# Another order of tasks in the mixer, at the first layer's end and in w_out of a hybrid decoder layer

## The chip, the cores and the metric

The kernel runs on one core of a Trainium2 chip. What counts is device time in microseconds (us) of one launch. The core has a matrix engine (TensorE, in the profile PE, with its weight loads as PEld), a vector engine (VectorE, DVE), a scalar engine (ScalarE, ACT), GpSimd (POOL) and a queue of transfers that SyncE (SP) issues. Each works through its own list of instructions in order, and they meet at semaphores.

## What is computed

One decoder layer on 512 tokens of width 1024, all in float32: a half-weighted SwiGLU feed-forward layer, a mixer of three branches, a projection `w_out`, and a second half-weighted feed-forward layer. Every step has a norm ahead of it and one behind it.

```python
x = x + 0.5 * rms_norm(swiglu(rms_norm(x)), ffn1_post)
u = rms_norm(x)
nsa_q, nsa_kv, nsa_g, dn_qkv, dn_a, dn_b, dn_z, mem_q = split(u @ w_in)
# NSA: compressed keys, selected blocks and window, 8 heads of 64
# DeltaNet: conv and silu of dn_qkv, then the chunked rule of 4 heads (chunks of 64):
#   a_mat = strict(beta * k k^T * decay) + I; solve a_mat against v and k; scan over chunks
#   o_dn = rms_norm(o_dn) * silu(dn_z)
# memory: cross attention of mem_q into 256 memory tokens
merged = sum(sigmoid(u @ w_gate[b]) * (o_b @ w_branch[b]) for b in 3 branches)
x = x + rms_norm(merged @ w_out)
x = x + 0.5 * rms_norm(swiglu(rms_norm(x)), ffn2_post)
```

## The kernel before

A float32 product is made of three products of rounded parts: every weight tile of 128x512 is loaded (`wraw`, in w_out `woraw`), ScalarE casts it to its high part `whi` (L106), VectorE or GpSimd subtracts that from the tile and leaves the low part `wlo` (L109), and TensorE multiplies high by high, low by high and high by low (L117 to L119, helper `mm3`). So each loaded tile costs a transfer, a cast, a subtraction and a dozen or so matmuls. `wload` holds four raw tiles in most stages; a load waits on SyncE's queue until one is free.

The program is a list of small tasks. `tasks` goes through lists of names in the table `PRM`, and calls one function for each name; the scheduler of the framework then interleaves their instructions, keeping what comes first in the lists ahead where it can. Three kinds of entry steer it: the lists (`order` for the mixer's first part, `order2` for attention and merge, `order0` for the first feed-forward layer's end, `order3` for w_out, `order_s` for the start), an offset of priority for a name (`off`, `off2` and so on), and for a name the number n such that every n-th low part goes to GpSimd instead of VectorE (`pool`, `pool3`; 0 is none).

The names in `order` that matter here: `c` is a product with `w_dn` and the convolution of one head and one of q, k, v (L185, L612: `cacc` from the product `pfm`); `h` its transposes and norm (`ptr`, then `rsqrt` L129 to L139, then `kn` or `qs`, then `ptk`); `k`, `r` and `l` make the tables of a head (`LT` is the lower triangle, from `pkk`); `z` is the product with `w_z`; `b` solves the triangle's 16x16 blocks for two heads at once: `LT` goes to DRAM (`dL`), comes back as `Lb`, 15 pairs of small VectorE steps (L719, L721) work on `Bi`, L722 turns it, and the result goes out (`dD`, from ScalarE's queue) and comes back as `Dc` (SyncE's queue, L726); `e` spreads `Dc` to `Dm` and `DT` (L739); `d` doubles the blocks in three levels (`pt`, `px`, `pxt`); `s` is the scan over chunks (`pst`, `pod`); `o` the output norm and its transposes (`on` L823, `pot` L824); `x` the tokens of the compressed keys (product with `w_cmp`, then 8 steps `X`, L900), `p` their hidden layer (`phid`, L917); `q` a product with `w_q`.

In `order0`: `k` and `v` are products with the memory's weights (`mem_k` gives `pfm`, `mem_v` gives `pmv`), each left by a copy on ScalarE (`mkv`, L517); `p`, `n`, `t` are post-norm, pre-norm (sum of squares on ScalarE, L152) and transposes (`ptr`, L166) of a half of the tokens. In `order3`: `s` splits the merged sum, `d` i h is half h of w_out's columns for token half i (accumulators `acc_mm` for d00, `acc_o` and `acc_r` for d01, `acc_e` for d10, `acc_s` for d11), and `p`, `n`, `t` are as above.

Of the kernel before, what the change touches and what calls it, by code (L numbers as in the profile page):

```python
# [33 lines left out]
PAD = 88  # L34


PRM = {'order': ['i', 'a', 'w', 'c01', 'h01', 'c00', 'c10', 'c02', 'r0', 'h00', 'h02', 'c12', 'k0', 'h10', 'c22', 'l0', 'c11', 'h11', 'h12', 'r1', 'z', 'k1', 'c21', 'l1', 'h22', 'b0', 'c20', 'h21', 'e0', 'r2', 'h20', 'c32', 'l2', 'c31', 'd00', 'h31', 'k2', 'r3', 'c30', 'd01', 'l3', 'b1', 'd02', 'x0', 's00', 'e1', 'd10', 'h32', 'x1', 'd11', 'h30', 's01', 's02', 's03', 'q0', 'p0', 'o0', 'k3', 'p1', 'q3', 'p2', 'p3', 'd12', 's10', 'p4', 'q1', 'p5', 's11', 'p6', 'p7', 's12', 'q2', 'f', 's13', 'o1'], 'dma': {'l': 'sync', 'b': 'sync', 'd': 'scalar', 'c': 'sync', 'r': 'sync'}, 'off': {'b0': 300, 'h31': 400, 'h00': 20, 'r1': 50, 'h32': 50, 'h11': 200, 'h12': 200, 'd10': 100, 'A01': 100, 'A10': 100, 'A11': 100, 'A20': 100, 'A31': 100, 'A21': 200, 'x0': 20, 'x1': 20, 'C2': 50, 'L': 200, 'S310': 400, 'S001': 20, 'S311': 400, 'A30': 100, 'r0': 400, 'd02': 20, 's11': 50, 'V20': 400, 'l3': 100, 'q1': 20, 'f': 400, 'l1': 20, 'h20': 100, 'h22': 100, 'r3': 50, 'P010': 100, 'y': 100, 'h02': 50, 'S101': 20, 'A00': 100, 'Q0': 50, 'Q1': 50, 'Q2': 50, 'Q3': 50, 'P110': 400, 'V31': 50, 'd01': 200, 'o0': 400, 'p0': 50, 'p1': 50, 'p2': 50, 'p4': 50, 'p5': 50, 'p6': 50, 'p7': 50, 'b1': 20, 'h01': 100, 'M15': 20, 'P201': 400, 'e0': 100, 'e1': 100, 'o1': 20, 'q0': 50, 'q2': 20, 'h21': 20, 'd11': 50, 'p3': 50}, 'ph': 'e', 'po': 'ss', 'xpd': (0, 1, 2), 'order2': ['K1', 'K0', 'B', 'M10', 'C3', 'Q0', 'C0', 'Q1', 'S000', 'S001', 'P001', 'C1', 'P000', 'S010', 'C2', 'S011', 'V00', 'P010', 'S100', 'P011', 'S110', 'Q2', 'V01', 'P100', 'S101', 'W0', 'P101', 'S111', 'Q3', 'M12', 'V10', 'P110', 'S200', 'P111', 'S210', 'V11', 'P200', 'M14', 'S201', 'M15', 'P201', 'S211', 'W1', 'V20', 'P210', 'M11', 'P211', 'V21', 'S301', 'S300', 'W2', 'P301', 'S311', 'P300', 'L', 'M13', 'S310', 'G0', 'V30', 'P310', 'G2', 'M16', 'P311', 'V31', 'W3', 'A00', 'M00', 'M17', 'A01', 'G1', 'U0', 'A10', 'M05', 'A11', 'G3', 'A30', 'A31', 'U1', 'U3', 'M03', 'A20', 'A21', 'U2', 'M07', 'M22', 'M02', 'M20', 'M24', 'M06', 'M27', 'M21', 'M01', 'M26', 'M23', 'M04', 'M25'], 'order0': ['d0', 'p0', 'n0', 't0', 'd1', 'k2', 'k0', 'p2', 'p3', 'k1', 'n1', 'v', 'k3', 't1'], 'order3': ['s2', 's3', 's7', 's6', 's1', 's5', 's0', 's4', 'd01', 'd00', 'g', 'p0', 'd10', 'n0', 't0', 'd11', 'p1', 'n1'], 't3': (('mm', 'r'), ('e', 's')), 'pool': {'W2': 2, 's13': 3, 'k0': 0, 'k1': 0, 'k2': 0, 'k3': 2, 'p3': 1, 'C0': 0, 'C1': 0, 'C2': 0, 'C3': 2, 'S310': 0, 'L': 3, 'd11': 3, 'p0': 1, 'p1': 1, 'p2': 1, 'p4': 2, 'p5': 1, 'p6': 1, 'p7': 1, 'S311': 0, 'h01': 0, 'h00': 0, 'h02': 0, 'h10': 0, 'h11': 0, 'h12': 0, 'h22': 0, 'h21': 0, 'h20': 0, 'h31': 0, 'h30': 3, 'h32': 0, 'i': 2, 'P011': 2, 'c21': 0, 'd01': 2, 'S000': 0, 'S001': 0, 'S010': 0, 'S011': 0, 'S100': 0, 'S101': 0, 'S110': 0, 'S111': 0, 'S200': 0, 'S201': 0, 'S210': 0, 'S211': 0, 'S300': 0, 'S301': 0, 'M24': 2, 'G2': 2, 'A01': 0, 'M10': 2, 'M15': 2, 'M12': 2, 'M14': 2, 'M13': 2, 'M17': 2, 'M11': 2, 'M16': 2, 'M23': 0, 'M27': 3, 'M01': 2, 'M00': 2, 'M03': 0, 'M07': 2, 'M06': 0, 'M22': 2, 'M04': 2, 'M20': 2, 'M26': 3, 'M02': 0, 'M21': 2, 'M25': 2, 'M05': 2, 'c11': 1, 'o1': 3, 'P000': 2, 'P001': 1, 'P010': 2, 'P100': 2, 'P101': 2, 'P110': 2, 'P111': 2, 'P200': 2, 'P201': 2, 'P210': 2, 'P211': 2, 'P301': 0, 'P300': 2, 'P310': 2, 'P311': 2, 'c12': 0, 'b1': 1, 'x0': 0, 'x1': 0, 'V21': 0, 'c30': 0, 'c01': 0, 'c02': 0, 'c00': 0, 'c10': 0, 'c22': 0, 'c20': 0, 'c31': 0, 'c32': 0, 's01': 3, 'A31': 0, 'd12': 0, 'y': 2, 'G0': 2, 'G1': 2, 'G3': 2, 'U3': 0, 'W3': 2, 'r1': 2, 's12': 3, 'U2': 0, 'Q0': 2, 'Q1': 2, 'Q2': 2, 'Q3': 1, 's00': 3, 's02': 2, 's03': 3, 's10': 3, 's11': 3, 'e1': 2, 'd00': 1, 'U0': 0, 'U1': 0, 'l2': 0}, 'pool3': {'d00': 3, 'd01': 3, 'd10': 3, 'd11': 3, 'p1': 2, 't1': 3, 't0': 3, 's5': 2, 's7': 2, 's1': 2, 's0': 2, 's3': 2, 's6': 2, 's2': 2, 's4': 2, 'q0': 1}, 'pool0': {}, 'off0': {'p3': 20, 'n1': 50, 't1': 100}, 'off3': {'s1': 20, 's5': 200, 'g': 200, 't0': 400}, 'tt': ('e', 's'), 'order_s': ['t00', 'w10', 'w00', 'y', 't01', 't02', 'w01', 't03', 'w11', 'R0', 'F000', 'x', 'F101', 'n', 'F200', 't10', 't11', 't12', 't13', 'c', 'F110', 'B', 'F211', 'F011'], 't0': ('e', 's'), 'rs': ((0, 0), (0, 0)), 'ra': (1, 1), 'warm': 8, 'pools': {'F000': 0, 'F101': 0, 'F200': 0, 'F011': 0, 'F110': 0, 'F211': 0, 'w10': 0, 'w11': 0, 't00': 0, 't01': 0, 't02': 0, 't03': 0, 't13': 0, 't10': 0, 't11': 0, 't12': 0, 'w00': 0, 'w01': 0}, 'ptc': 'vvs', 'cva': 'v', 'offs': {'t13': 100, 'R1': 400}, 'vnc': 's', 'sp3': 0, 'hsc': 'vv', 'sf2': 2, 'psc': 'vvvv', 'sp1': 0, 'vbs': 'v', 't1c': 'vs', 'sgv': 256}


class Body:  # L40
    def __init__(self, ctx, tc, a, out, tap):
# [17 lines left out]
        pw = self.bank("o", "warm")  # L59
        for _ in range(PRM.get("warm", 10)):  # L60
            nc.tensor.matmul(pw, wm[:, :P], wm, start=True, stop=True)
# [204 lines left out]
    def ffn_tile(self, n, f, t, xh, xl, RB, H, banks=None, tags=("mm", "mm"), pre=None):  # L266
# [14 lines left out]
        if r:  # L281
            (nc.vector if w <= PRM["sgv"] else nc.gpsimd).tensor_tensor(sg[:, :r], sg[:, :r], RB, op=OP.mult)
        return nc.vector.tensor_tensor(H[:, f, t], sg, pu, op=OP.mult)
# [320 lines left out]
    def dn_conv(self, h, s, uh, ul):  # L604
# [4 lines left out]
        ac = self.tp.tile([P, SEQ], F32, tag="tmpa", bufs=2, name="cacc")  # L609
        self.scale(PRM.get("cva", "s"), ac, p, self.cw[:, j, 3:4])  # L610
        for i in range(3):
# [11 lines left out]
    def dn_head(self, h, s, y, sc, dp, d):  # L623
# [7 lines left out]
        if s == 2:  # L631
            d["vb"] = dp.tile(T4, F32, tag="vb", name="vb", bufs=4)
            if PRM.get("vbs", "v") == "v":
                v.tensor_tensor(d["vb"], p, beta[:, :, h, None].to_broadcast(T4), op=OP.mult)
# [11 lines left out]
        n = self.da.tile(T4, F32, tag="kn", name="kn", bufs=1) if s else self.tp.tile(T4, F32, tag="tmpb", name="qs", bufs=2)  # L646
        if PRM.get("hsc", "vv")[s] == "v":
            v.tensor_tensor(n, p, r[:, :, None].to_broadcast(T4), op=OP.mult)
# [53 lines left out]
    def dma(self, k):  # L702
        return getattr(self.nc, PRM.get("dma", {}).get(k, "sync"))

# [789 lines left out]
```

## Time and profile before

| | |
|---|---|
| three runs | 1382.18, 1367.98, 1378.45 us; median 1378.45 |
| profiled execution | 1365.18 us, its span 1363.4 us |
| PE busy | 1332.1 us (98%) |
| DVE, ACT, POOL busy | 897.0, 719.1, 146.1 us |
| mean granted TensorE clock | 0.996 |

The span runs from the first to the last instruction; the execution's own time has 1.8 us around it. The stages lie so: the first feed-forward layer to 370, memory products and norms to 397, the mixer's first part to 638, attention and merge to 955, w_out to 1004, the second feed-forward layer to the end. The first head pair's blocks are solved at 486 to 521, the second's at 541 to 575.

### The profile page before, as it was taken

Reading aid. Unit: us, or ns where it says so; the run is one execution under the profiler, and the core shown is the slowest. Engines: PE = TensorE matmul, PEld = TensorE weight load, DVE = VectorE, ACT = ScalarE, POOL = GpSimd, SP = SyncE. Lnnn points to the kernel's source line nnn. Section 1 sums busy time; section 2 is a strip of 40 time slices with the busy share of each in tenths; the row PEclk is TensorE's granted clock in tenths of the full one; section 3 lists DMA queues with packets and bytes.
Section 4 is the critical chain, followed back from the end, with each engine's and each line's share of the span. In section 5 each row is a group of like instructions: output and inputs, shape, how many; then the busy total and the mean of one; then the engine's idle time right before and its main releaser. Section 6 shows DMA issues by size and latency. Waiting matters only on the chain.

```text
span 1363.4 us, 21808 instructions
## 1 busy us (share of the span) xinstructions
PE 1332.1 (98%) x7839; PEld 1130.3 (83%) x7839; DVE 897.0 (66%) x1797; ACT 719.1 (53%) x1542; POOL 146.1 (11%) x132
## 2 busy tenths in 40 slices
PE   9999999999999999999999999999999999999997
PEld 8889999787887878677777777888788899998886
DVE  6897875777558576646876424223587778766765
ACT  7556664766555553216654334323585565646643
POOL 0020000000011312003110121333300000000000
PEclk9999999999999999999999999999999999999999
DMA  7643331676654332423121222532744433317673
GB/s 254 194 147 109 109 110 32 209 244 209 190 176 125 98 100 63 113 82 118 46 63 47 70 63 92 164 100 93 243 136 148 134 121 98 121 33 261 194 224 101
DMA packets 107453, 178.32 MB, mean 131 GB/s; under 512 B 18908, under 2 KB 28496, under 8 KB 107344
## 3 DMA queue, kind: packets, MB, share of 16 engines
q1 hardware_dynamic: 107056, 176.67, 41.8%
q8 instruction: 61, 1.00, 0.3%
q14 instruction: 48, 0.39, 0.1%
q10 hardware_dynamic: 288, 0.26, 0.1%
HBM read 166.84 MB, written 10.01 MB: 130 GB/s over the span
## 4 chain that ended last, share of the span: by engine, by line
PE 49%; DVE 3%; ACT 1%; issue 1%; DVEq 0%; ACTq 0%
PE pfm L119 5%; PE pfm L117 5%; PE pfm L118 5%; PE smm L406 5%; PE se L406 3%; PE po L1051 2%; PE ss L406 2%; PE ps L1019 2%; PE ppt L1039 1%; PE acc_mm L117 1%; PE acc_mm L118 1%; PE acc_mm L119 1%; PE acc_e L118 1%; PE acc_e L117 1%; PE acc_e L119 1%; PE acc_s L117 1%
## 5 line engine op out<-in xcount | busy, mean ns | idle before, releaser
L106 ACT CAST whi<-wraw 128x512 fp32r<-128x512 f32 (+1 forms) x314 | 189.8, 616 | 185.3 <-PE pfm L119 70.3
L109 DVE TENSOR_TENSOR wlo<-wraw,whi 128x512 fp32r<-128x512 f32 (+1 forms) x270 | 184.1, 690 | 143.6 <-ACT whi L106 139.6
L118 PE MATMUL pfm<-xth,wlo 128*128 128x512 f32 x384 | 154.9, 405 | 2.6 <-DVE wlo L109 2.6
L117 PE MATMUL pfm<-xth,whi 128*128 128x512 f32 x384 | 155.7, 406 | 1.1 <-DVE drz L134 0.7
L119 PE MATMUL pfm<-xtl,whi 128*128 128x512 f32 x384 | 154.0, 402 | 0.0
L118 PEld LDWEIGHTS pfm<-xth,wlo 128*128 128x128 f32 x384 | 72.3, 189 | 19.3 <-DVE wlo L109 3.2
L117 PEld LDWEIGHTS pfm<-xth,whi 128*128 128x128 f32 x384 | 72.4, 189 | 18.5 <-issue 3.9
L119 PEld LDWEIGHTS pfm<-xtl,whi 128*128 128x128 f32 x384 | 72.4, 189 | 15.4 <-issue 1.0
L109 POOL TENSOR_TENSOR wlo<-wraw,whi 128x512 fp32r<-128x512 f32 (+1 forms) x41 | 51.1, 1246 | 243.0 <-ACT whi L106 196.4
L106 ACT CAST ringh<-ringr 128x512 fp32r<-128x512 f32 x82 | 50.1, 620 | 42.4 <-DMA ringr<-in_ffn_d_dram 11.2
L406 PE MATMUL smm<-thi,fset 128*128 128x256 f32 x384 | 69.5, 279 | 0.0
L109 DVE TENSOR_TENSOR wlo<-ringr,ringh 128x512 fp32r<-128x512 f32 x75 | 51.4, 689 | 21.8 <-PE acc_e L119 8.7
L406 PEld LDWEIGHTS smm<-thi,fset 128*128 128x128 f32 x384 | 58.5, 188 | 0.2
L422 DVE TENSOR_TENSOR up<-smm,s 128x256 f32<-128x256 f32 x32 | 13.6, 424 | 67.2 <-ACT se L419 67.2
L406 PE MATMUL smm<-thi,fxtl 128*128 128x256 f32 x192 | 53.6, 279 | 0.6 <-DVE fxtl L388 0.6
L406 PE MATMUL smm<-thi,fxth 128*128 128x256 f32 x192 | 53.3, 278 | 0.0
L406 PE MATMUL se<-thi,fset 128*128 128x256 f32 x256 | 46.7, 280 | 0.0
L1022 ACT ACTIVATE Pm<-Pm,nm 128x128 f32<-128x128 f32 (+1 forms) x64 | 35.6, 557 | 11.9 <-DVE nm L1021 11.6
L258 POOL TENSOR_TENSOR xb<-xb,pre 128x512 f32<-128x512 f32 x2 | 2.5, 1277 | 356.7 <-ACT pre L257 356.7
L123 DVE TENSOR_TENSOR Hl<-H,Hh 128x256 fp32r<-128x256 f32 x88 | 35.0, 420 | 7.0 <-ACT Hh L122 5.5
L406 PEld LDWEIGHTS se<-thi,fset 128*128 128x128 f32 x256 | 39.1, 187 | 0.0
L379 DVE TENSOR_TENSOR fs<-fq 128x1024 f32<-128x1024 f32 x32 | 38.9, 1217 | 0.0
(550 smaller groups left out, 3979.3 us busy)
## 6 DMA issues: line engine op xcount, KB each, us to landing
wraw<-in_ffn_d_dram SPq DMA_DIRECT2D x94, 256.0 KB, 2.9
ringr<-in_ffn_d_dram SPq DMA_DIRECT2D x82, 256.0 KB, 2.9
fq<-in_ffn_g_dram SPq DMA_DIRECT2D x64, 256.0 KB, 2.9
fq<-in_ffn_u_dram SPq DMA_DIRECT2D x64, 256.0 KB, 2.7
wraw<-in_w_gate_dram SPq DMA_DIRECT2D x48, 256.0 KB, 2.8
wraw<-in_ffn_u_dram SPq DMA_DIRECT2D x34, 256.0 KB, 3.2
wraw<-in_ffn_g_dram SPq DMA_DIRECT2D x34, 256.0 KB, 3.5
woraw<-in_w_out_dram SPq DMA_DIRECT2D x32, 256.0 KB, 2.9
```

The lines of the kernel that those rows point to most:

```text
L106: nc.scalar.copy(hi, raw)
L109: eng.tensor_tensor(lo, raw, hi.bitcast(F32), op=OP.subtract)
L117: t.matmul(out, lh, rh, start=first, stop=False)
L118: t.matmul(out, ll, rh, start=False, stop=False)
L119: t.matmul(out, lh, rl, start=False, stop=last)
L123: return self.nc.vector.tensor_tensor(lo, src, hi.bitcast(F32), op=OP.subtract)
L379: add = lambda *x: v.tensor_tensor(*x, op=OP.add)
L406: m = lambda x, y, **kw: te.matmul(out, x, y, skip_group_check=True, **kw)
L1019: te.matmul(s[:, : max(n, 256)], A[:, qb * P : qb * P + P], K[j][:, : max(n, 256)], start=j == 0, stop=j == 1)
L1022: nc.scalar.activation(pm, pm, AF.Exp, bias=nm[:, qb : qb + 1], scale=-1.0, accum_out=sm[:, qb : qb + 1])
L1039: te.transpose(pt[:, o : o + P], Pm[:, self.OFF[qb] + kb * P : self.OFF[qb] + kb * P + P], self.ident)
L1051: te.matmul(po[64 * g : 64 * g + 64, kb * P :], vt[:, kb, br * P + 64 * g : br * P + 64 * g + 64], pts[g][:, col[kb] : col[kb] + n], start ...
```

## The change

It changes the table and nothing else. The tasks, their tiles and their arithmetic stay; the order of their instructions, and in a few products which engine subtracts, are others. The lists, cut to what moves most (the rest of the line is the table's other entries):

```diff
-'l0', 'c11', 'h11', 'h12', 'r1', 'z', 'k1', 'c21', 'l1', 'h22', 'b0', 'c20', 'h21', 'e0',
+'c11', 'h12', 'h11', 'h22', 'r1', 'k1', 'l1', 'b0', 'c21', 'z', 'h21', 'e0', 'c20',
...
-'k2', 'r3', 'c30', 'd01', 'l3', 'b1', 'd02', 'x0', 's00', 'e1', 'd10', 'h32', 'x1', 'd11',
+'k2', 'r3', 'd01', 'l3', 'b1', 'd02', 'x0', 's00', 'e1', 'd10', 'c30', 'h32', 'x1', 'd11',
...
-'q0', 'p0', 'o0', 'k3', 'p1', 'q3', 'p2', 'p3', 'd12',
+'q0', 'q3', 'p0', 'o0', 'p1', 'p2', 'p3', 'k3', 'd12',
...
-'order0': ['d0', 'p0', 'n0', 't0', 'd1', 'k2', 'k0', 'p2', 'p3', 'k1', 'n1', 'v', 'k3', 't1']
+'order0': ['d0', 'p0', 'n0', 't0', 'd1', 'k2', 'k0', 'p2', 'p3', 'v', 'k3', 'n1', 'k1', 't1']
...
-'order3': ['s2', 's3', 's7', 's6', 's1', 's5', 's0', 's4', 'd01', 'd00', 'g', 'p0', 'd10', 'n0', 't0', 'd11', 'p1', 'n1']
+'order3': ['s3', 's7', 's2', 's6', 's1', 's5', 's0', 's4', 'd00', 'd01', 'd11', 'g', 'p0', 'n0', 't0', 'd10', 'p1', 'n1']
...
-'off0': {'p3': 20, 'n1': 50, 't1': 100}, 'off3': {'s1': 20, 's5': 200, 'g': 200, 't0': 400}
+'off0': {'p3': 20, 'n1': 50, 'd0': 200, 'k2': 400, 'k1': 400}, 'off3': {'s1': 20, 's5': 200, 'g': 200, 't0': 400, 'd10': 200, 'p0': 200}
```

`order2` has about twenty names moved by one to five places; in `off` the offsets of `b1`, `s00`, `Q1`, `M14` rise to 200, of `A20` and `P011` to 400; `offs` gives two weight loads and transposes of the start an offset. In `pool` the names `h00`, `d02` and `V00` get 2, `K1` 3, `C0`, `M10` and `M06` 1, `G3` and `V11` 0; in `pool3` `d11` goes from 3 to 0. GpSimd subtracts for 51 tiles before and for 50 now (10 and 7 of them in w_out).

VectorE at the first head pair's blocks (`b0`), the last steps. Before:

```order
L719 TENSOR_TENSOR Bt<-Lb,Bi 64x28
L129 TENSOR_SCALAR drm<-dss 128x4
L612 SCALAR_TENSOR_TENSOR cacc<-pfm,cw,cacc 128x509
L721 TENSOR_TENSOR Bi<-Bi,Bt 64x2x14
L130 TENSOR_SCALAR dry<-drm 128x4
L612 SCALAR_TENSOR_TENSOR cacc<-pfm,cw,cacc 128x510
L719 TENSOR_TENSOR Bt<-Lb,Bi 64x15
L133 TENSOR_TENSOR drz<-dry 128x4
L612 SCALAR_TENSOR_TENSOR cacc<-pfm,cw,cacc 128x511
L721 TENSOR_TENSOR Bi<-Bi,Bt 64x15
```

Now:

```order
L719 TENSOR_TENSOR Bt<-Lb,Bi 64x48
L721 TENSOR_TENSOR Bi<-Bi,Bt 64x4x12
L719 TENSOR_TENSOR Bt<-Lb,Bi 64x39
L721 TENSOR_TENSOR Bi<-Bi,Bt 64x3x13
L719 TENSOR_TENSOR Bt<-Lb,Bi 64x28
L721 TENSOR_TENSOR Bi<-Bi,Bt 64x2x14
L109 TENSOR_TENSOR wlo<-wraw,whi 128x512
L719 TENSOR_TENSOR Bt<-Lb,Bi 64x15
L721 TENSOR_TENSOR Bi<-Bi,Bt 64x15
L722 COPY Bi<-Bi 64x256
```

The convolutions and the norm of other heads, which stood between the steps, now stand behind them; four subtractions are left among the thirty steps, and in TensorE's list w_z's product stands beside them.

ScalarE at the memory products, around 380 us. Before:

```order
L517 COPY mkv<-pfm 128x256
L106 CAST whi<-wraw 128x512 x3
L152 ACTIVATE junk,ss<-xb 128x1024
L517 COPY mkv<-pfm 128x256
L106 CAST whi<-wraw 128x512
L152 ACTIVATE junk,ss<-xb 128x1024
```

Now:

```order
L517 COPY mkv<-pfm 128x256
L106 CAST whi<-wraw 128x512 x4
L152 ACTIVATE junk,ss<-xb 128x1024
L106 CAST whi<-wraw 128x512 x2
L152 ACTIVATE junk,ss<-xb 128x1024
L106 CAST whi<-wraw 128x512
L517 COPY mkv<-pmv_4269 128x512
```

No copy of a `mem_k` product stands between the two sums of squares any more; two casts do, and a copy of a `mem_v` product comes behind them.

SyncE's queue at the second head pair's blocks, from the load of `Lb` to that of `Dc` (`w` are the tiles of the compressed keys' hidden layer). Before:

```order
L712 DMA Lb<-dL_5685 64x16x16
L912 DMA w_6391<-in_cmp_w_dram 128x512
L105 DMA wraw<-in_w_q_dram 128x512 x2
L912 DMA w_6435<-in_cmp_w_dram 128x512
L912 DMA w_6437<-in_cmp_w_dram 128x512
L912 DMA w_6443<-in_cmp_w_dram 128x512
L912 DMA w_6445<-in_cmp_w_dram 128x512
L912 DMA w_6495<-in_cmp_w_dram 128x512
L726 DMA Dc<-dD_5920 128x16x16
```

Now:

```order
L712 DMA Lb<-dL_5685 64x16x16
L105 DMA wraw<-in_w_q_dram 128x512
L912 DMA w_6361<-in_cmp_w_dram 128x512
...
L912 DMA w_6434<-in_cmp_w_dram 128x512
L726 DMA Dc<-dD_5876 128x16x16
L912 DMA w_6495<-in_cmp_w_dram 128x512
L912 DMA w_6497<-in_cmp_w_dram 128x512
L105 DMA wraw<-in_w_q_dram 128x512 x2
```

The hidden layer's first loads stood ahead of `Lb` before; now all eight of its first tiles (the rows left out are six of them) stand between the two loads of the chain, and the next two behind it.

## Rows read from the trace of the kernel before

**Rows 1.** First part of the page: busy time, share and instructions by engine

```profile
PE 1332.1 (98%) x7839; PEld 1130.3 (83%) x7839; DVE 897.0 (66%) x1797; ACT 719.1 (53%) x1542; POOL 146.1 (11%) x132
```

**Rows 2.** Waits of PE: us in total, times, longest

```profile
PE pfm L118 <- DVE wlo L109: 2.6, 1, 2.6
...
PE pmv L117 <- ACT mkv L517: 1.4, 1, 1.4
PE pot L824 <- DVE on L823: 1.2, 1, 1.2
```

**Rows 3.** Windows, first PE's busy us of each, then PEld, DVE, ACT, POOL, PEclk, DMA

```profile
370.00:397.00 27.00, 25.25 (x161) 21.75 (x160) 21.09 (x55) 16.59 (x36) 2.09 (x4) 1.00 0.63 189
...
500.00:521.00 21.00, 18.03 (x89) 13.88 (x88) 18.58 (x55) 10.27 (x29) 5.23 (x6) 1.00 0.45 126
548.00:566.00 18.00, 15.38 (x72) 9.94 (x73) 13.28 (x59) 3.37 (x8) 1.27 (x1) 0.91 0.28 86
541.50:580.06 38.56, 35.86 (x183) 24.08 (x182) 25.31 (x91) 11.15 (x40) 3.14 (x3) 0.96 0.44 115
...
984.00:1000.00 16.00, 13.55 (x63) 9.92 (x62) 14.30 (x30) 11.41 (x25) 4.37 (x3) 1.00 0.38 133
1000.00:1026.00 26.00, 24.06 (x176) 22.13 (x176) 22.05 (x55) 21.66 (x47) 0.00 (x0) 1.00 0.44 142
```

**Rows 4.** Timeline of ACT at 380 us: start, us, engine, line, operation, [idle before]

```profile
380.87 1.06 ACT L152 ACTIVATE junk<-xb 128x1024 bf16<-128x1024 f32 x1 [1.81 <-DVE xb L260]
```

**Rows 5.** Timeline of DVE at the first head pair's blocks

```profile
486.44 0.68 DVE L700 TENSOR_TENSOR LT<-pkk,dec 128x512 f32<-128x512 f32 x1
...
493.89 0.17 DVE L719 TENSOR_TENSOR Bt<-Lb,Bi 64x15 f32<-64x15 f32 x1 [1.05 <-DMA Lb<-dL]
...
512.36 0.37 DVE L722 COPY Bi<-Bi 64x256 f32<-64x256 f32 x1
...
519.90 2.15 DVE L739 TENSOR_TENSOR Dm<-Dc,msk 128x512 f32<-128x512 f32 x2 [1.98 <-DMA Dc<-dD]
```

**Rows 6.** Two matmuls of 512 columns, back to back; VectorE's splits (the page's groups)

```profile
518.11 0.39 PE L119 MATMUL pfm<-xtl,whi 128*128 128x512 f32 x1
518.34 0.39 PE L117 MATMUL pfm<-xth,whi 128*128 128x512 f32 x1
...
L109 DVE TENSOR_TENSOR wlo<-wraw,whi 128x512 fp32r<-128x512 f32 (+1 forms) x270 | 184.1, 690 | 143.6 <-ACT whi L106 139.6
```

**Rows 7.** Timeline of DVE at the second head pair's blocks

```profile
540.81 0.68 DVE L700 TENSOR_TENSOR LT<-pkk,dec 128x512 f32<-128x512 f32 x1
...
548.38 0.16 DVE L719 TENSOR_TENSOR Bt<-Lb,Bi 64x15 f32<-64x15 f32 x1
...
557.82 0.21 DVE L721 TENSOR_TENSOR Bi<-Bi,Bt 64x55 f32<-64x55 f32 x1
561.87 0.35 DVE L801 SCALAR_TENSOR_TENSOR S<-S,gl,pst 128x128 f32<-128x128 f32 x1 [3.85 <-PE pst L798]
...
565.77 0.38 DVE L722 COPY Bi<-Bi 64x256 f32<-64x256 f32 x1
...
573.65 2.15 DVE L739 TENSOR_TENSOR Dm<-Dc,msk 128x512 f32<-128x512 f32 x2 [0.45 <-DMA Dc<-dD]
...
579.66 2.15 DVE L823 SCALAR_TENSOR_TENSOR on<-pod,dory,zg 128x128 f32<-128x128 f32 x8
```

**Rows 8.** PE's groups in 541.5 to 580.06: count, busy us, mean ns, idle before

```profile
L118 PE MATMUL pfm<-xth,wlo 128*128 128x512 f32 x21 | 8.8, 425 | 2.6 <-DVE wlo L109 2.6
```

**Rows 9.** Timeline of POOL and DVE at 626 us

```profile
626.18 1.29 POOL L109 TENSOR_TENSOR wlo<-wraw,whi 128x512 fp32r<-128x512 f32 x1 [6.84 <-ACT whi L106]
...
626.24 1.25 DVE L134 TENSOR_TENSOR dorz<-dorz,dorm 128x8 f32<-128x8 f32 x1
```

**Rows 10.** Timeline of w_out: ACT behind d00's end, PE's transposes

```profile
976.23 0.60 ACT L211 ACTIVATE junk<-acc_mm 128x512 bf16<-128x512 f32 x1 [0.24 <-PE acc_mm L119]
...
995.16 0.95 PE L166 MATMUL ptr<-cst,xa 128*128 128x128 f32 x6 [1.33 <-DVE xa L155]
```

2 lines of the change are left out of this document (1 added, 1 removed).

## The prediction, made before the run

> **What bounds the kernel now.** I read the page's busy times first: TensorE is busy 1332.1 of 1363.4 us [rows 1], so all its waits together are 31.3 us, and no new order can save more than that and what the clock loses. The reader should see that VectorE's 66% is then no limit by itself; it counts only where one of its results comes last. So the second view is the list of TensorE's waits [rows 2]: single waits of 1 to 3 us, each in another place. The third is the windows, which give TensorE's idle time around each place, the clock with it [rows 3]. The change touches six of these places. Last I read the timelines there, to see what stood in front of the late result, and the orders of both kernels, to see what stands there now.
>
> All sums are against the profiled execution, 1365.18 us, of which 1.8 lie around the span. The median of the three runs is 1378.45, 13 us above it, and the runs lie 14 us apart; I take it that the change moves both by the same amount, and forecast the median.
>
> **The change part by part.**
>
> *The memory products (order0).* TensorE is idle for 1.75 us in 370 to 397 [rows 3], 1.4 of it one wait of `pmv` for the copy of a `mem_k` product [rows 2]. That copy stood behind a sum of squares on ScalarE (L152), and the sum had itself waited 1.81 us for VectorE [rows 4]. In the new order no such copy stands between the sums. What comes behind them is two casts and a `mem_v` copy, with seven matmuls or more of other work queued. I take -1.4, with bounds 0 (the cast behind L152 is now the late one) and -1.75.
>
> *The first head pair's blocks.* In 500 to 521 TensorE is idle for 21.00 - 18.03 = 2.97 us [rows 3], at the end for `Dm`, which waits for `Dc` [rows 5]. The chain: `LT` is done at 487.1; `Lb` is there at 493.9, 6.8 later; the thirty steps last until 512.7, 18.8; `Dm` starts at 519.9, 7.2 behind them [rows 5]. The steps are small, 0.16 to 0.21 us each [rows 7], and 30 of them at some 0.25 from start to start are 7.5; the other 11 us are convolutions, norms and splits in between. Now three splits at 0.7 (less where they overlap, 0.6) stand between them behind the first pairs, so 7.5 + 1.8 + 0.4 for L722 = 9.7. The new cost: VectorE waits at `Dm` for `Dc`, and behind that, in order, stand a convolution step and the split which a third product wants (c32, behind c21 and c20). Counted from `LT`'s end, VectorE has that split at 6.8 + 9.7 + 7.2 + 2.8 (three spreads) + 1.4 = 27.9. TensorE comes to it after 64 matmuls of w_z, 48 of two convolution products and one more at 0.23 each [rows 6], 26.0, and 0.9 of transposes, 26.9. So 1.0 us of waiting remains: 1.0 - 2.97, say -2.0. Bounds: -3.0 (nothing is late) and +1 (the transfers take 3 us more).
>
> *The second head pair's blocks and the compressed keys.* Here the window 548 to 566 shows 18.00 - 15.38 = 2.62 us idle and a granted clock of 0.91, which is 1.6 us more [rows 3]; the wait is one split of 2.6 us [rows 2], queued behind sixteen `X` steps and the first pairs of the substitution. In the new order the two w_cmp products end 24 matmuls of c30 and their own apart, and w_q's splits stand ahead of the second eight `X`. That wait goes. But the chain through this pair now decides more. It runs from `LT` (done 541.5) by the first step at 548.4 (6.9), the last at 566.15 (17.8), `Dm` at 573.65 (7.5) to `on` at 579.66 (6.0) [rows 7], and `pot`, which wants `on`, stands in TensorE's list ahead of the rest. Of the 17.8, VectorE was held 3.85 for `pst` [rows 7], so 13.9 without. From the fastest to the slowest that the two pairs showed, the chain is 6.8 + 13.9 + 7.2 + 6.0 = 33.9 to 6.9 + 18.8 + 7.5 + 6.0 = 39.2. TensorE's work beside it before: 35.86 us busy in 183 records, less 1.5 for the clock of 0.96 [rows 3], is 34.3; of these 61 are 512-column matmuls (21, 20 and 20 [rows 8]) at 0.23 [rows 6], 14.0, so the other 122 cost 0.166 each. In the new order I count 74 large ones and 52 small ones between `LT` and `pot`; of the small, 48 (hidden layer and scan) make two records each, as before, so 104 at 0.166: 17.0 + 17.3 = 34.3. If the hidden layer's matmuls, now more of them in a row, cost less, it is down to 29. I take the chain at 35, one us above its low end, since no held time is expected and some splits are; then 0.7, say 1.0 us, of waiting remains, at `pot`, and with it no gap as long as that of 3 us ahead of the slow stretch. That is 1.0 - 2.62 - 1.6 = -3.2. Bounds: -4.2, and 39.2 - 29 = 10 us of waiting, with the slow stretch kept, +7.4.
>
> Two transfers follow each other between L722 and `Dm`, and the trace has them at 7.2 and 7.5 us [rows 5, 7]. The Trainium skill, "DMA: Bandwidth & Descriptors", section "Latency and other measured facts", puts the fixed cost of a DMA at about 2 us; by that the two would be some 4 us, an estimate from that page, and `pot` would never wait. The rows have nearly twice that, and they decide.
>
> *The second output norm (o1).* `pot` waits 1.2 us there [rows 2], behind 23 large matmuls of w_k. In the new order 18 cover it: 5 x 0.23 = +1.15, with bounds 0 and +2.5.
>
> *w_out.* Before, d01 came first, then d00, and from d00's end at 976.23 to the transposes of the first token half at 995.16 [rows 10] it was 18.9 us, against 66 matmuls of w_out. The window 984 to 1000 has 2.45 us idle [rows 3], 1.33 of it at these transposes [rows 10]. Now d00's two sums and gains are done while d01 runs, and d01 ends last. From there only 55 matmuls, 12.7 us, stand ahead of the transposes. The chain loses the two sums of `acc_mm` and one more behind them (1.7, at 0.6 each [rows 10]), two gains of `acc_e` on VectorE (1.2) that stood in it, and d11's GpSimd splits. Such a split takes 1.29 us, and a tiny VectorE step that meets one takes 1.25 us [rows 9] where its neighbours take under 0.2; I count two of these in the old chain, 2.2 us. That leaves 18.9 - 1.7 - 1.2 - 2.2 = 13.8, a wait of 1.1, a gain of 1.3. The other half pays it back: `acc_e` now ends last, and its two sums and gains come to the second chain, whose window (1000 to 1026) already has 1.94 idle [rows 3]; +1.3. I take 0, with bounds -2 and +5 (the first chain keeps its 18.9).
>
> The Trainium skill, "SBUF — State Buffer", section "Who interferes with whom", says that a VectorE instruction with two inputs from SBUF contends with a GpSimd one that reads there, and that the later may block entirely. The row of 1.25 us agrees. It speaks against the new splits on GpSimd in attention (K1, C0, M10, M06); by it, each could hold a VectorE step for a us, and if all four were last for TensorE the sum would be 4 us worse. GpSimd has one split fewer in all.
>
> *What else moves.* Attention and merge, the start and the transposes of the first layer's other half get another order, and in each a wait of half a us may come or go; the start loads the same bytes ahead of the second tokens. New waits are likelier than fewer, since the old order had few there: +1.5, with bounds -1 and +4.
>
> The sum: -1.4 - 2.0 - 3.2 + 1.15 + 0 + 1.5 = -3.95, say -4. On the profiled execution that is 1361.2; on the median, **1374.5 us**.
>
> **The rivals.** *All gains come and no loss.* The two chains are hidden, w_out saves its 1.3 to 2, nothing new appears: -1.75 - 3.0 - 4.2 - 1.3 = -10, 1368. For it speaks that the new order puts splits earlier than their products in the places I counted; against it, that two waits on `Dc` now have something behind them.
>
> *The second pair's chain becomes the bound: slower.* SyncE's queue has eight tiles of the hidden layer and then `Dc`, which waits for the chain; two further tiles and w_q's weights stand behind it, and `on` stands behind `Dm` on VectorE. From a chain of 38 us on, against 34.3 of work, the place costs more than it did; at 39.2 and work of 29 it costs +7.4 instead of -3.2, and the whole is +6.6, 1385. For it: VectorE needs the `X` steps and the scan's updates between the thirty steps, which before took 17.8. Against it: 3.85 of these were a hold that may not come back.
>
> *w_out's transposes stand in front of too little work.* The chain keeps its 18.9 us against 12.7: 6.2 us waiting where 2.45 was, and 1.3 for the second half, +5 and so +1 in all, 1379.5. Against it: three of its pieces are gone by the order.
>
> **How the numbers follow.** The forecast has 0.5, all gains 0.2, the second pair 0.2, w_out 0.1. The cases lie between 1368 and 1385; the three runs lie some 7 us to either side of their middle, which the range must take in: 1361 to 1388. About 1%, 13.8 us, is what a measurement of this kernel can tell from no change. Faster by more than that (under 1364.7) asks for all gains and a low median, 0.14; slower (above 1392.2) for the second pair's case or several losses and a high one, 0.07; the rest is 0.79.
>
> **What would show it.** The list of waits should have no `pmv` on `mkv` and no `pfm` on a split of 2 us or more in the mixer; the thirty steps of the first pair should take under 11 us. `pot` ahead of the second pair's levels should wait under 2 us and the clock stay at 1.0 there; if it waits 5 or more, the slower rival holds. In w_out the transposes `ptr` should wait about 1 us. The prediction is wrong if TensorE's idle total is not 2 to 6 us below 31.3, above all if attention and merge, whose order I followed least, has gained waits.

## The result, and the profile after

| | runs | median, us | from | to |
|---|---|---|---|---|
| before | 15 | 1378.45 | 1365.58 | 1382.18 |
| changed | 15 | 1362.09 | 1358.24 | 1364.00 |

The changed kernel takes 0.9908 of the time over all runs (95% interval 0.9881 to 0.9936), 0.9% less; the two medians alone give 0.988. The profiled execution took 1360.61 us with a span of 1358.8, against 1365.18 before: 4.6 us less, where the prediction had 4. The medians lie 16.4 us apart. Both numbers are right, for the runs of before are on two levels, 6 of the 15 at 1365.6 to 1370.7 and 9 at 1377.8 to 1382.2, with nothing between; its profiled execution is one of the lower, its median one of the upper. The changed kernel has one level. (Before's runs in the experiments below also show a few times in between.) So there are two questions: where the 4.6 us come from, and what took the upper level away.

The page's busy times of the changed kernel, which answer to [rows 1]:

```profile
PE 1331.6 (98%) x7839; PEld 1127.5 (83%) x7839; DVE 898.5 (66%) x1798; ACT 718.6 (53%) x1540; POOL 144.8 (11%) x131
```

TensorE is as busy as before; its idle time fell from 31.3 to 27.2. The waits of TensorE, for [rows 2] (us in total, times, longest):

```profile
PE pfm L117 <- DVE cacc L612: 3.0, 1, 3.0
...
PE pkk L699 <- POOL kbT L677: 1.3, 2, 0.8
...
PE pfm L118 <- POOL wlo L109: 1.0, 1, 1.0
...
PE ptm L117 <- ACT whi L106: 0.8, 1, 0.8
...
PE pot L824 <- DVE on L823: 0.4, 1, 0.4
```

The three waits of [rows 2] are gone or small: the split of 2.6, `pmv` on `mkv`, and most of `pot`. The wait of the first pair's doubling for `Dm`, 1.68 us before, is gone as well. The four others shown are new, the longest of them at the first head pair, where the prediction had a gain. The windows of the same places, for [rows 3] (TensorE's busy us first, its clock third from the end):

```profile
370.00:397.00 27.00, 27.00 (x171) 23.37 (x171) 21.13 (x56) 17.55 (x39) 2.10 (x4) 1.00 0.65 203
500.00:521.00 21.00, 18.01 (x100) 15.33 (x98) 16.55 (x34) 9.43 (x19) 3.50 (x4) 0.92 0.29 89
548.00:566.00 18.00, 17.89 (x105) 13.86 (x104) 16.36 (x65) 7.16 (x19) 1.27 (x1) 1.00 0.35 90
980.00:1000.00 20.00, 18.88 (x89) 14.44 (x89) 16.47 (x35) 14.63 (x31) 2.58 (x2) 1.00 0.33 110
1000.00:1026.00 26.00, 24.00 (x195) 23.10 (x194) 22.98 (x56) 22.54 (x48) 0.00 (x0) 1.00 0.54 177
```

Idle time at the memory products went from 1.75 to 0, and at the second pair from 2.62 to 0.11 with the clock up from 0.91 to 1.00. At the first pair it is 2.99 where it was 2.97, and the clock, which was 1.00 there, is 0.92. So on this level the second pair pays, and the first costs.

One part of the 4.6 us is not of the change. The first 50 us, before and then now:

```profile
0.00:50.00 50.00, 46.62 (x336) 42.38 (x337) 38.48 (x85) 33.72 (x71) 0.89 (x8) 0.97 0.67 222
0.00:50.00 50.00, 46.70 (x337) 41.26 (x337) 39.09 (x85) 33.82 (x71) 0.89 (x8) 1.00 0.68 224
```

0.03 of 50 us are 1.5 us of clock. But this share differs from execution to execution: it is 1.00 in the trace of "w_out only" below and 0.93 in that of "c30 moved", which have the start of before, and 0.93 in that of "start only", which has the new one.

VectorE at the first pair's blocks, for [rows 5]:

```profile
482.35 0.17 DVE L719 TENSOR_TENSOR Bt<-Lb,Bi 64x15 f32<-64x15 f32 x1 [0.47 <-DMA Lb<-dL]
...
490.81 0.37 DVE L722 COPY Bi<-Bi 64x256 f32<-64x256 f32 x1
...
497.11 3.00 DVE L739 TENSOR_TENSOR Dm<-Dc,msk 128x512 f32<-128x512 f32 x2
500.04 1.78 DVE L739 TENSOR_TENSOR DT<-Dc,msk 128x512 f32<-128x512 f32 x1
501.75 0.74 DVE L185 TENSOR_SCALAR cacc<-pfm,cw 128x512 f32<-128x512 f32 x1
...
505.04 0.74 DVE L612 SCALAR_TENSOR_TENSOR cacc<-pfm,cw,cacc 128x511 f32<-128x511 f32 x1
```

The thirty steps and the turn take 8.8 us (18.8 before), with three subtractions between them in the trace. Then the spreads hold VectorE from 497.11 to 501.75, 4.6 us, and the convolution stands behind them. TensorE meanwhile:

```profile
502.55 0.39 PE L119 MATMUL pfm<-xtl,whi 128*128 128x512 f32 x1
505.93 0.77 PE L117 MATMUL pfm<-xth,whi 128*128 128x512 f32 x1 [2.99 <-DVE cacc L612]
506.49 0.63 PE L118 MATMUL pfm<-xth,wlo 128*128 128x512 f32 x1
...
508.94 0.39 PE L119 MATMUL pfm<-xtl,whi 128*128 128x512 f32 x1
```

A product waits 2.99 us until the convolution of an earlier product has read its `pfm`. Behind the wait the matmuls take 0.63 us where they take 0.39 otherwise: the clock is at its lower level, for some three us.

VectorE at the second pair's blocks, for [rows 7]:

```profile
542.69 0.69 DVE L700 TENSOR_TENSOR LT<-pkk,dec 128x512 f32<-128x512 f32 x1
...
549.55 0.17 DVE L719 TENSOR_TENSOR Bt<-Lb,Bi 64x15 f32<-64x15 f32 x1
...
564.54 0.37 DVE L722 COPY Bi<-Bi 64x256 f32<-64x256 f32 x1
...
572.27 0.69 DVE L739 TENSOR_TENSOR Dm<-Dc,msk 128x512 f32<-128x512 f32 x1 [5.81 <-DMA Dc<-dD]
...
576.98 2.15 DVE L823 SCALAR_TENSOR_TENSOR on<-pod,dory,zg 128x128 f32<-128x128 f32 x8
```

From `LT`'s end at 543.4 to `on` it is 33.6 us, of which the steps take 15.0 and the way to `Dm` 7.4; the forecast had 35. In w_out ([rows 10]) the transposes wait 1.1 us in either half:

```profile
988.36 0.55 PE L166 MATMUL ptr<-cst,xa 128*128 128x128 f32 x3 [1.08 <-DVE xa L155]
...
1013.26 1.09 PE L166 MATMUL ptr<-cst,xb 128*128 128x128 f32 x8 [1.09 <-DVE xb L155]
```

### The profile page after: what moved, and what is told of

It is laid out like the page before. It is cut to its first block, busy times and chain, and to the rows that moved or that the text cites. A ratio compares the mean times of both kernels' runs of the same rounds, so it can differ in the third digit from the quotient of the medians.

```text
span 1358.8 us, 21807 instructions
## 1 busy us (share of the span) xinstructions
PE 1331.6 (98%) x7839; PEld 1127.5 (83%) x7839; DVE 898.5 (66%) x1798; ACT 718.6 (53%) x1540; POOL 144.8 (11%) x131
## 4 chain that ended last, share of the span: by engine, by line
PE 88%; DVE 5%; DMA 2%; ACT 2%; issue 1%; POOL 0%; SPq 0%; ACTq 0%; DVEq 0%; POOLq 0%
PE smm L406 10%; PE pfm L117 7%; PE pfm L118 7%; PE pfm L119 7%; PE se L406 7%; PE ss L406 3%; PE po L1051 2%; PE ps L1019 2%; PE acc_e L118 2%; PE acc_e L117 2%; PE acc_e L119 2%; PE sr L406 2%; PE acc_s L119 1%; PE acc_s L117 1%; PE acc_s L118 1%; PE so L406 1%
```

## The experiments

Each kernel is timed against the kernel before, in three groups of four (in the table's order), each group on one chip. Over the 99 runs beside them the kernel before was 51 times on the lower level (six of these stand between, at 1369.4 to 1373.3 with clocks of .990 to .993) and 48 times on the upper (clocks .982 to .988); the medians of its levels were 1365.5 and 1380.0 us in the first group, 1366.4 and 1379.7 in the second, 1365.1 and 1378.5 in the third. The last two columns give the number of runs on a level, their median and their clocks; the difference is to the lower level of before in the same group.

| kernel | median, us | ratio, 95% interval | lower level (difference) | upper level |
|---|---|---|---|---|
| before again | 1377.64 | 1.0012 (.9968 to 1.0057) | 4: 1365.6 (+0.1), .995 to .998 | 8: 1378.4, .984 to .986 |
| mixer only | 1363.52 | .9917 (.9878 to .9955) | 12: 1363.5 (-2.0), .994 to .997 | none |
| w_out only | 1364.70 | .9985 (.9937 to 1.0033) | 7: 1363.3 (-2.2), .994 to .997 | 5: 1377.5, .984 to .985 |
| start only | 1373.49 | .9990 (.9946 to 1.0034) | 6: 1367.6 (+2.0), .993 to .999 | 6: 1378.5, .983 to .988 |
| c30 moved | 1373.38 | .9976 (.9935 to 1.0017) | 5: 1361.6 (-4.8), .995 to .999 | 7: 1374.6, .986 to .989 |
| b0 early | 1366.81 | .9947 (.9917 to .9976) | 12: 1366.8 (+0.4), .995 to .999 | none |
| all but the mixer | 1373.05 | .9987 (.9945 to 1.0029) | 6: 1365.2 (-1.2), .994 to .997 | 6: 1379.1, .984 to .986 |
| spreads two and two | 1361.21 | .9908 (.9873 to .9943) | 10: 1361.2 (-5.2), .996 to .999 | none |
| both moves | 1362.47 | .9934 (.9896 to .9972) | 10: 1362.5 (-2.6), .995 to .998 | none |
| prefix back | 1369.96 | 1.0004 (.9972 to 1.0036) | 10: 1370.0 (+4.9), .990 to .993 | none |
| b0 half way | 1374.77 | 1.0017 (.9981 to 1.0052) | none | 10: 1374.8, .986 to .989 |
| without attention | 1359.18 | .9907 (.9871 to .9942) | 10: 1359.2 (-5.9), .995 to .999 | none |

**Before again.** The kernel before, without an edit, to see whether the levels are its own.

> The kernel before, unchanged. Its 15 runs lie on two levels, 6 at 1365.6 to 1370.7 and 9 at 1377.8 to 1382.2, and the profiled one (1365.18) is of the lower. Theory one: the upper level is one stage that goes wrong by some 13 us in some executions, so half of the runs are at 1366 and half at 1380 again, and a trace of the upper level has the 13 us within one or two stages. Rival: the level is of the chip and the moment (clock or memory over the whole span); then the runs next to each other share a level, and a trace of the upper one is longer by 1% in every stage.

They are: 4 runs on the lower, 8 on the upper, 12.8 us apart. The profiled execution was one of the lower level, so the trace that was to show the place is still missing here.

**Mixer only.** The kernel before with the changed kernel's `order`, and the offsets and shares of its lower-case names:

```diff
-'r1', 'z', 'k1', 'c21', 'l1', 'h22', 'b0', 'c20', 'h21', 'e0',
+'h22', 'r1', 'k1', 'l1', 'b0', 'c21', 'z', 'h21', 'e0', 'c20',
...
-'k2', 'r3', 'c30', 'd01',
+'k2', 'r3', 'd01',
...
-'d10', 'h32',
+'d10', 'c30', 'h32',
```

> Only the mixer's first part in the new order (its list, its offsets and shares); the rest as before. By the two traces the mixer's first part is 1.3 us shorter on the lower level. Theory one with its seat in the mixer: no run above 1372, ratio 0.991 to 0.994. Seat elsewhere, or the rival: both levels remain, ratio 0.999.

One level, 1363.5. The upper level is decided in the mixer's first part; on the lower one the mixer is worth 2 us. The rival of "before again", a level of the chip and the moment, does not hold either: the runs of before in the same group were 18 times on the lower level and 17 times on the upper, and none of these 12 was.

**w_out only.** `order3`, `off3` and `pool3` of the changed kernel, the rest as before:

```diff
-'s4', 'd01', 'd00', 'g', 'p0', 'd10', 'n0', 't0', 'd11', 'p1', 'n1'
+'s4', 'd00', 'd01', 'd11', 'g', 'p0', 'n0', 't0', 'd10', 'p1', 'n1'
```

> Only w_out in the new order (list, offsets and shares); the rest as before. By the two traces the stage gains about 2 us on the lower level. Theory one with its seat in w_out or behind it: no run above 1372, ratio about 0.990. Otherwise both levels remain and the ratio is 0.998 to 0.999.

Both levels stay, each some 2 us lower than before's. w_out is a gain of its own.

**Start only.** The two new offsets of `offs`.

```diff
-'offs': {'t13': 100, 'R1': 400}
+'offs': {'t13': 100, 'R1': 400, 't03': 20, 'w10': 200}
```

> Only the start's two offsets changed. By the two traces the first stage gains 0.6 us. Theory one with its seat at the start (granted clock 0.97 in the first 50 us before, 1.00 after): no run above 1372, ratio about 0.991. Otherwise both levels remain and the ratio is 0.9995.

Both levels stay; the lower is 2 us higher with six runs from 1364.1 to 1369.5, too wide a spread to read a cost or the expected gain of 0.6 from. The profiled one, 1369.1, had a clock of 0.93 in its first 50 us.

**c30 moved.** One move in the kernel before, which takes the wait of 2.6 us for the split away:

```diff
-'r3', 'c30', 'd01', 'l3', 'b1', 'd02', 'x0', 's00', 'e1', 'd10', 'h32',
+'r3', 'd01', 'l3', 'b1', 'd02', 'x0', 's00', 'e1', 'd10', 'c30', 'h32',
```

> The kernel before with one name moved: c30 behind d10, as in the new order. Then the two w_cmp products lie apart and w_q's splits stand ahead of the second eight X steps, so the wait of 2.8 us at 551 should go. The runs of before show a granted clock of 0.995 to 0.998 on the lower level and 0.982 to 0.987 on the upper: the upper level is a long stretch at half clock. Theory one: that stretch starts at this wait, which lies just ahead of the thinnest part of the mixer. Then no run above 1372 and a ratio of 0.990 to 0.993. Rival: it starts at the waits of the first head pair (500 to 521); then both levels stay and the lower one gains 2 to 4 us.

Each level falls by some 5 us: the wait and its slow stretch are worth what [rows 3] say, 2.62 + 1.6, and a little more. But 7 of 12 runs are on the upper level. My theory, that the upper level starts at this wait, falls.

**b0 early.** The other large move alone:

```diff
-'r1', 'z', 'k1', 'c21', 'l1', 'h22', 'b0',
+'r1', 'k1', 'l1', 'b0', 'z', 'c21', 'h22',
```

> The kernel before with k1, l1 and b0 moved ahead of c21 and z, as in the new order; the two w_cmp products still end together. Theory one: both levels remain, since the wait of 2.8 us is there still; the lower one changes by -2 to +1. Rival (the long stretch starts at the first pair's waits): no run above 1372.

The rival holds: no run is on the upper level, and the lower one is not lower. This move takes the upper level away and gains nothing else.

**All but the mixer.** Attention, the first layer's end, w_out and the start as in the changed kernel, the mixer's entries as before.

```diff
-order2, order0, off0, order3, off3, pool3, offs, upper-case names of off and pool: before's
+the same entries: the changed kernel's
```

> The new kernel with the mixer's first part as before. Both levels remain if the seat is in the mixer alone; the lower level is some 3 us under that of before (by the two traces: 0.6 at the start, 0.9 at the first layer's end and the memory products, 2 in w_out and behind it), so runs at 1363 and at 1376.

The levels are back, six runs on each; the lower is 1.2 us under before's, where 3 were expected. And its profiled execution, 1378.92 us, is one of the upper level, the only one of those here. TensorE's wait there and the windows (columns as in [rows 3]):

```profile
521.64 1.10 PE L761 MATMUL pt<-Dm,LT 128*128 128x64 f32 x8 [1.55 <-DVE Dm L739]
```

```profile
518.00:520.00 2.00, 2.00 (x11) 1.39 (x8) 1.02 (x2) 1.10 (x2) 1.64 (x2) 1.00 0.55 61
520.00:522.00 2.00, 0.45 (x4) 0.36 (x4) 1.10 (x2) 1.94 (x10) 1.24 (x2) 1.00 0.57 139
522.00:524.00 2.00, 1.94 (x14) 1.62 (x14) 1.99 (x3) 1.47 (x3) 0.50 (x1) 0.91 0.00 0
524.00:526.00 2.00, 2.00 (x9) 1.81 (x9) 1.17 (x4) 0.00 (x0) 0.00 (x0) 0.50 0.00 0
...
548.00:550.00 2.00, 2.00 (x16) 1.78 (x16) 0.97 (x2) 0.00 (x0) 0.00 (x0) 0.50 0.00 0
550.00:552.00 2.00, 2.00 (x13) 1.72 (x12) 0.84 (x2) 1.36 (x2) 1.43 (x2) 0.77 0.31 91
```

and those of the kernel before, on the lower level, with the same list of the mixer's tasks:

```profile
520.64 1.11 PE L761 MATMUL pt<-Dm,LT 128*128 128x64 f32 x8 [1.68 <-DVE Dm L739]
```

```profile
518.00:520.00 2.00, 0.97 (x5) 0.44 (x3) 0.10 (x1) 1.60 (x6) 0.61 (x3) 1.00 0.91 180
520.00:522.00 2.00, 1.36 (x9) 1.08 (x9) 2.00 (x3) 1.92 (x6) 1.50 (x1) 1.00 0.01 2
522.00:524.00 2.00, 1.93 (x16) 1.81 (x15) 1.74 (x6) 0.16 (x1) 0.00 (x0) 1.00 0.00 0
524.00:526.00 2.00, 2.00 (x17) 1.91 (x16) 1.42 (x7) 0.00 (x0) 0.31 (x1) 1.00 0.28 49
```

Both wait for the first pair's `Dm`, 1.55 us in the run of the upper level and 1.68 in that of the lower. Behind it the kernel before goes on at 1.00, and in the run of the upper level the clock is at 0.50 from 523.6 to 550.9 (0.91 and 0.77 are the shares of the first and the last window). 27 us at half the clock lose 13.5 us, and the two levels of this kernel are 13.9 apart: the upper level is this stretch. This is one trace; the other five runs of the level have its clock, .984 to .986.

**Spreads two and two.** The changed kernel with the third spread on GpSimd and without `e0`'s offset, against the wait of 2.99:

```diff
-'xpd': (0, 1, 2)
+'xpd': (0, 1)
...
-'e0': 100,
```

> The new kernel with two instead of three of the four spreads of Dc on VectorE (the others on GpSimd), and without e's offset. In the new kernel the spreads hold VectorE for 4.6 us, a convolution stands behind them, and TensorE waits 3.1 us at 502.6 for the bank that it frees. With one spread less ahead of the convolution that wait should fall to 0 to 1.5 us: -1.5 to -3 us on the new kernel, ratio to before 0.988 to 0.990. Rival: GpSimd's two spreads are now what pt or px waits for, 1 to 3 us, and nothing is gained.

5.2 us below before's lower level, where the changed kernel was 4.4 below (1362.09 against 1366.5, the median of the six runs of before on it). A shorter wait stands in the place of the long one, and the clock stays up:

```profile
505.82 0.66 PE L630 MATMUL ptr<-cst,cy 128*128 128x128 f32 x4 [1.50 <-ACT cy L614]
```

```profile
500.00:521.00 21.00, 19.50 (x117) 16.77 (x116) 16.78 (x35) 9.52 (x20) 6.51 (x7) 1.00 0.31 101
```

That is 1.5 us less idle and 1.7 less lost to the clock than in the changed kernel's window. But the kernel gained only 0.8 to 0.9, where 1.5 to 3 were expected; some of the 3.2 comes back elsewhere. In this trace the clock of the first 50 us was 0.93, and no run shows what else it is.

**Both moves.** The diffs of "c30 moved" and "b0 early" together, in the kernel before.

```diff
-'r1', 'z', 'k1', 'c21', 'l1', 'h22', 'b0', ... 'r3', 'c30', 'd01', ... 'd10', 'h32',
+'r1', 'k1', 'l1', 'b0', 'z', 'c21', 'h22', ... 'r3', 'd01', ... 'd10', 'c30', 'h32',
```

> Two moves in the list of the kernel before and nothing else: k1, l1 and b0 right behind r1 (as in the run with the first pair's blocks early), and c30 behind d10 (as in the run with only c30 moved). Theory (the long half-clock stretch starts at the first pair's waits, and the 2.6-us wlo wait is a cost of its own): the gains add. No run on the upper level, clocks of the runs .995 or more, times between 1360 and 1366, median near 1362.5 (1366.8 with b0 alone, less 3.5 to 4 for c30). It would thus match the changed kernel within a microsecond or so with two of its moves. Rival (the rest of the mixer's order is needed as well): median 1365 or above, or runs near 1376.

1362.47, as expected, and one level. But the gains do not add: against before's lower level in their own groups the moves gave -4.8 and +0.4 alone and -2.6 together. Two moves of the list give all but some 2 us of what the whole change gives.

**Prefix back.** The changed kernel with its list up to `h21` as before:

```diff
-'c11', 'h12', 'h11', 'h22', 'r1', 'k1', 'l1', 'b0', 'c21', 'z', 'h21', 'e0', 'c20', 'r2',
+'c11', 'h11', 'h12', 'r1', 'z', 'k1', 'c21', 'l1', 'h22', 'b0', 'c20', 'h21', 'e0', 'r2',
```

> The changed kernel with the list of the mixer's tasks up to b0 and h21 written as before (k1, l1 and b0 behind z and c21 again); every other part of the change stays, c30's place, w_out, the first layer's end and the start too. Theory (it is the place of the first pair's blocks that takes the upper level away): the upper level is back, in a third to two thirds of the runs near 1372 to 1377 with clocks of .985 to .989, the others near 1360 to 1363. Rival (the upper level went through the sum of the change's moves, or its start needs the exact queue of the kernel before): one level, 1360 to 1364.

Neither: one level, at 1370, with clocks between the two. The trace shows two long waits with a short slow stretch behind each:

```profile
502.63 0.77 PE L117 MATMUL pfm<-xth,whi 128*128 128x512 f32 x1 [5.80 <-DVE Bi L721]
...
524.42 1.87 PE L761 MATMUL pt<-Dm,LT 128*128 128x64 f32 x8 [2.28 <-DVE Dm L739]
```

```profile
524.00:528.00 4.00, 3.58 (x17) 3.49 (x17) 4.00 (x6) 0.00 (x0) 1.87 (x2) 0.57 0.03 7
528.00:532.00 4.00, 4.00 (x16) 3.50 (x17) 0.56 (x3) 2.13 (x3) 0.00 (x0) 0.58 0.00 0
532.00:536.00 4.00, 4.00 (x34) 3.79 (x32) 1.81 (x4) 0.58 (x2) 0.31 (x1) 1.00 0.22 66
```

Behind the second, the longer of the waits for `Dm` seen here, the clock is back after some seven us. In this list five matmuls of 512 columns stood in a row in between; in the run of the upper level there were never more than three while its clock was low. So the old place of `b0` does not bring the upper level back in every list: here the rest of the changed mixer, its later list and its offsets, stands around it.

**b0 half way.** In the kernel before:

```diff
-'z', 'k1', 'c21', 'l1', 'h22', 'b0',
+'z', 'k1', 'l1', 'b0', 'c21', 'h22',
```

> Half a dose in the kernel before: k1, l1 and b0 ahead of c21 and h22 but still behind z. TensorE's list then has the q/k transposes, the first product, the convolution's transposes and the first two doublings of the pair back to back, with the 9 product matmuls between them taken out: the wait for the spreads stands in one piece instead of three, and no shorter in all. Theory (the long stretch starts where TensorE is idle for one to three microseconds and then has only the pair's short matmuls): the upper level stays, in a third or more of the runs, near 1376 to 1380; the lower level 1363 to 1368. Rival (only the last wait at 519.7 in its place behind two others starts it): one level.

All ten runs have the low mean clock, where a third or more was expected; the median is a little under the expected 1376 to 1380. In the trace it begins at the same place, behind the waits for `Dm` (1.59 and 0.35 us), and stays for 24 us:

```profile
517.79 1.10 PE L761 MATMUL pt<-Dm,LT 128*128 128x64 f32 x8 [1.59 <-DVE Dm L739]
```

```profile
516.00:520.00 4.00, 2.05 (x16) 1.72 (x14) 2.95 (x3) 0.79 (x1) 2.91 (x2) 0.98 0.37 82
520.00:524.00 4.00, 4.00 (x18) 3.52 (x18) 1.96 (x4) 1.99 (x9) 0.51 (x2) 0.50 0.00 0
...
540.00:544.00 4.00, 4.00 (x18) 2.89 (x17) 2.24 (x4) 0.62 (x1) 0.00 (x0) 0.54 0.12 34
544.00:548.00 4.00, 4.00 (x36) 3.54 (x36) 2.14 (x4) 0.96 (x2) 2.23 (x2) 1.00 0.35 101
```

What the kernel before does in half of its runs, this order, without the nine products between the transposes and the second doubling, does in all.

**Without attention.** The changed kernel with before's `order2` and upper-case names of `off` and `pool`, and the spreads two and two.

```diff
-'xpd': (0, 1, 2), 'e0': 100, order2 and upper-case names: the changed kernel's
+'xpd': (0, 1), order2 and upper-case names: before's
```

> The changed kernel without its change to the attention's tasks (order2 and the upper-case names of off and pool as before), and with the first pair's spreads on two engines that are free there (no priority for e0, xpd (0,1)). The attention part gave back 0.4 us by the marks, the spreads' variant was at 1361.21. If these are what they seem: 1360.3 to 1361.2 at the median, one level, clocks .996 or more. If the attention's change costs nothing: 1361.2 or above.

1359.18, the fastest of all and 1.1 us below the expected range: 5.9 us below the lower level, where "spreads two and two" was 5.2 below. That the change to attention costs 0.7 us is not more than the levels differ from group to group (1.3), so it stays open.

The traces of all these kernels agree on one thing, which goes further than the single edits. Where `b0` stands early (the changed kernel, "mixer only", "b0 early", "both moves", and the two with two and two spreads), TensorE has no wait for `Dm` at the first pair, and none of their runs is on the upper level. Where it stands late, TensorE waits for `Dm` there, 1.2 to 2.3 us at a time, and all these kernels but "prefix back" have the upper level.

## Why the prediction was right and wrong

The forecast of 1374.5 was 12.4 us too high. The measured median lies inside the range, 1.1 us from its lower end, and 0.9% is within its 1%. But 1362.09 is also under 1364.7, the line that the forecast drew for "faster" and gave 0.14. It said that this asks for all gains and a low median; not all gains came, and the level did it. The signs it named came out: no `pmv` on `mkv`, no split of 2 us in the mixer, the steps of the first pair under 11 us, a clock of 1.00 at the second, about 1 us at w_out's transposes, and 4.1 us less idle time. None of them looks at the levels. By its steps:

*The level.* The step that failed is "the runs lie 14 us apart; I take it that the change moves both by the same amount, and forecast the median". The gap was there to be read: two runs near 1380, one at 1368 and a profiled execution of 1365 are two levels of one program, and it was the profiled one that the sum described. The upper level is 27 us at half the clock behind the first pair's waits, and moving `b0` takes it away. Shown by "b0 early" and "both moves" (0 of 22 runs on it), the kernel before (half of its runs) and "b0 half way" (10 of 10). Moving `b0` is enough in the list of before; that it is the only way is not shown, for "prefix back" has it in the old place and has no upper level. For the median the term was worth -12.0 (from 1378.45 to 1366.5, the lower level of before), where the prediction had 0; the other 4.4 of the 16.4 us are the gain on the lower level.

*The sum* fits the profiled execution, -4.6 for -4, but in part by errors that cancel, which is luck:

| step | forecast | measured in the profiled executions |
|---|---|---|
| memory products | -1.4 | -1.75, idle time 0 |
| first pair | -2.0 | +1.7: idle 2.97 to 2.99, and 0.08 of 21 us to the clock |
| second pair, compressed keys | -3.2 | -4.1: idle -2.5, clock -1.6 |
| second output norm | +1.15 | -0.8: `pot` waits 0.4 in all, for 1.2 |
| w_out | 0 | -1.3 in the first half, +0.1 in the second |
| what else moves | +1.5 | about +1.5, the rest to -4.6, with new waits of 1.3 (`pkk`), 1.0 (`pfm` on GpSimd's split) and 0.8 (`ptm`), and with the 1.5 us of clock at the start in its favour, which are of the execution and not of the change; without them it would be +3 |

The gain at the *memory products* is the order's: TensorE is idle for 0.0 us in this window in all five traces with the new `order0`, and for 1.6 to 2.0 in the nine others.

At the *first pair* the steps took 8.8 us where 9.7 were forecast; the way to `Dm` is 5.9 from L722's end and shows no wait for `Dc`. But the wait named was the wrong one: not a split behind the spreads, but a product whose buffer a convolution had to read first, also behind them. And "three spreads, 2.8" was 4.6: at 496.74 to 501.28 GpSimd had three instructions in a row, and the spreads beside them took 1.5, 1.5 and 1.8 us, where before one of three took 1.5 and the others 0.7. The second of the three on GpSimd:

```profile
498.06 1.51 POOL L739 TENSOR_TENSOR DT<-Dc,msk 128x512 f32<-128x512 f32 x1
```

"Spreads two and two" shows what the wait and its clock cost in this window, 3.2 us, of which 0.8 to 0.9 arrived in the time. I had also left out that such a wait takes the clock with it, though [rows 3] had that at the second pair. And the early place has a price in front: a wait of 0.6 to 0.9 us for `kbT` at the first pair's tables stands in every trace with `b0` early (0.85 in the changed kernel, part of the 1.3 for `pkk`) and in none with it late.

At the *second pair* the mechanism was right and the chain well sized, 33.6 for 35, and the wait of 1.0 that was to remain at `pot` is not there. (Of the work beside it, 52 small matmuls of which 48 make two records are 100 records and not 104; that makes 33.6 us for 34.3.) "c30 moved" shows the gain by itself. The rival in which this chain becomes the bound does not hold, nor the one in which w_out's transposes stand in front of too little work: they wait 1.08 us, as forecast (1.1). In *w_out* it was the payback of 1.3 in the second half that did not come, and "w_out only" gives the same 2 us on both levels.

What stays open: why the same list of the mixer, with waits for `Dm` of 1.55 and 1.68 us, has the clock go down behind them in one execution and not in the other; why "prefix back", with a wait of 2.28 us, comes out of the slow stretch in seven us; what ended the long stretch; and which part of the order beyond the two moves gives the last 2 us.

## What to carry to other kernels

When the runs of a kernel lie on two levels, ask first which of them the profile is of, and compare the granted clocks: a change can move the share of runs on a level, and here that was worth 12.0 us of the median where everything else gave 4.4. A wait of two us in front of a row of short matmuls is to be priced with what the clock may lose behind it, not at its own length. The price of an instruction depends on what runs beside it: a spread took 0.7 us alone and 1.5 to 1.8 beside GpSimd.

## What the runs showed of the hardware

TensorE was busy 2.00 of 2.00 us in every window from 524 to 550 in the run of the upper level, and its clock stayed at 0.50 for all of it. The Trainium skill, "TensorE: Matmul & The Clock Gate", Part 1, says that activity releases the throttle, and that the number of slow matmuls at the start of a kernel differs from run to run. The second agrees (the clock of the first 50 us is 0.93 to 1.00 in the traces here), and the runs show the same in the middle of a kernel (51 of 99 runs of one program on one level, 48 on the other). The first agrees behind the changed kernel's wait, where after 2.99 us of idle time the clock was back in some three us. It does not agree in the run of the upper level: after a wait of 1.55 us the clock took 27 us of full windows to come back.

A tiny VectorE step took as long as the GpSimd instruction beside it: 1.25 us for L719 on 64x15, which takes 0.17 elsewhere. A step with one input did so too:

```profile
563.05 1.25 DVE L719 TENSOR_TENSOR Bt<-Lb,Bi 64x15 f32<-64x15 f32 x1
...
572.88 1.03 DVE L129 TENSOR_SCALAR dorm<-oss 128x8 f32<-128x8 f32 x1
```

```profile
563.01 1.27 POOL L690 TENSOR_TENSOR qdT<-qT,eg 128x512 f32<-128x512 f32 x1 [19.81 <-ACT qT L656]
...
572.38 1.50 POOL L739 TENSOR_TENSOR DT<-Dc,msk 128x512 f32<-128x512 f32 x1 [8.11 <-DMA Dc<-dD]
```

Both end with the GpSimd instruction, at 564.3 and 573.9.
